# Second product of each attention score over 128 rows instead of 64, in a hybrid decoder step on Trainium2

## Chip, cores and metric

One Trainium2 chip, of which the kernel uses one core: TensorE (PE) for matrix products, VectorE (DVE), ScalarE (ACT) and GpSimd (POOL) for elementwise work, and DMA queues. The metric is the time of one execution on the device in microseconds (us). Three runs of the kernel before took 1948.69, 1954.34 and 1954.75 us; the median is 1954.34.

## The reference, cut to what matters

One layer of a decoder for 1024 prompt tokens and 8 samples of 4 tokens, model width 1024: RMSNorm, one combined projection, three parallel mixers (sliding-window attention, a gated short convolution, a gated delta net), gates and an output projection, then a gated MLP with a convolution, and a final norm. The change touches the attention of the prompt alone: 8 query heads share 2 key/value heads of 64 features, in blocks of 128 queries against 256 keys (the block's own and those of the block before):

```python
s = jnp.einsum('bnqhgd,bnkhd->bnhgqk', q, k) * (HEAD_DIM ** -0.5)
s = jnp.where(mask[None, :, None, None], s, -jnp.inf)
m = jnp.maximum(jnp.max(s, axis=-1, keepdims=True), sink)
p = jnp.exp(s - m)
p = p / (jnp.sum(p, axis=-1, keepdims=True) + jnp.exp(sink - m))
o = jnp.einsum('bnhgqk,bnkhd->bnqhgd', p, v)
```

All inputs are float32.

## The kernel before

**Products in two parts.** TensorE multiplies in float32r, which carries 12 significant bits of a number. A float32 operand is therefore split into a high and a low part (`split`, lines 215 to 218: ScalarE copies the high part, VectorE or GpSimd subtracts it from the source). A projection (`products`, line 320, matmuls on line 326) makes three products for each of 8 k tiles: w high with x high, w high with x low, w low with x high. Each product is a weight load (the operand that stays in the array, 128 x 128) and a matmul of 352 columns. Three PSUM banks serve the projections, five the other work.

**Order of the work.** A list of jobs (`ORDER`) gives the order of the projections. Between their matmuls, at every few of them, `bg.tick()` lets one of several lanes of background work issue a step: the delta net's scan, the attention, sums for later stages. A lane waits at its `yield` for a condition or an estimated time. The order of instructions on each engine is fixed when the program is built; a planner that simulates times orders them by priority (`schedule_with_timeline_sim=True`). While the program runs, an engine takes its instructions in that order, each as soon as its semaphores allow.

**The stages around the change.** Attention runs as background from about 545 to 825 us of the span, beside the projections z (of the delta net) and most of the gates. `attn_blocks` (line 1559) prepares each of the 8 blocks: it loads q and k of the block twice, into partitions 0 to 63 and 64 to 127 (lines 1571, 1572), then builds the operands. `qs` has q's high part in the upper 64 partitions (0 to 63) and q's low part in the other 64 (lines 1579, 1580). `kk[:, 0:512]` has k's high part in both halves (line 1581, ScalarE). `kk[0:64, 512:1024]` has k's low part in the first half alone (line 1582, GpSimd). Lines 1584 and 1585 do the same for v.

`units` (line 1595) are three lanes that take 16 units, one for each block and key/value head. A unit has four query heads, in two pairs; a pair shares one PSUM bank. For each head, line 1612 multiplies all 128 rows of `qs` with k's high part (q high and q low with k high in one product) and line 1613 adds the product of 64 rows, q high with k low. So a pair is a group of four matmuls with 256 columns each, with 128, 64, 128 and 64 rows. Then follow, mostly on VectorE and ScalarE, the mask (line 1616), maximum, exponentials (line 1625) and the normalisation (line 1630); TensorE transposes the result (line 1642), it is split, and line 1653 multiplies it with v. Lines 1657 and 1658 add the parts of the output, which goes to DRAM.

Behind attention, `h_build` (line 1774) prepares sums of h for the last gates in four rounds: additions on line 1789 (VectorE and GpSimd), subtractions on lines 1803 and 1812 (VectorE), and splits of the results. Line 1203 is the evacuation of projections on VectorE.

Of the kernel before, what the change touches and what calls it, by code (L numbers as in the profile page):

```python
# [7 lines left out]
F32R = mybir.dt.float32r  # L8
AF = mybir.ActivationFunctionType
ALU = mybir.AluOpType  # L10
# [4 lines left out]
D = 1024          # model width  # L15
KD = 8            # k tiles of the model width
SEQ = 1024
NB = 8            # prompt blocks (attention) and chunks (delta net) of 128 tokens
NS = 32           # sample tokens, column SEQ + b * 4 + t
T = SEQ + NS  # L20
TG = 352          # token group of one PSUM bank
# [9 lines left out]
TICK_US, UNTIL_US, DMA_US, MAX_BUSY_US = 0.45, 0.3, 2.5, 8.0   # estimates: a tick, one of a wait, a transfer's latency, a full queue  # L31
SLOT = 1084       # words of one SBUF slot
N_COL, N_BG = 24, 18
PRI_EVAC, PRI_PAIR = 100, 100
PRI_SPLIT = 200                   # how far ahead of their place in the program weights are split

# columns of the constant array
# [4 lines left out]
def shape_constants():  # L42
    """Identity, triangles and masks: they depend on the shapes alone."""
# [31 lines left out]
class Lanes:  # L75
    """Background work, traced in steps between the matrix products of the projections."""
# [10 lines left out]
    def after(self, us):  # L87
        """true us from now"""
        t = self.now + us
        return lambda: self.now >= t  # L90

    def arrived(self):
        """true when the transfers issued so far should be over"""
        return self.after(max(self.busy - self.now, 0) + DMA_US + 0.9)
# [27 lines left out]
class Arena:  # L122
    """SBUF slots of one size; a slot is free again after its tile's last use."""
# [27 lines left out]
XT_ACT = 1, 4, 7   # k tiles whose x^T the scalar engine copies  # L151
# [22 lines left out]
def trunk(tc, A, O, cst_d):  # L174
# [25 lines left out]
    def banks(n):  # L200
        """true when a lane may keep n more PSUM banks over its steps"""
        return lambda: held[0] + n <= limit[0]
# [12 lines left out]
    def split(src, hi, lo, eng):  # L215
        """hi + lo == src exactly, each in the 12 significant bits that float32r carries."""
        nc.scalar.copy(hi, src)  # L217
        eng.tensor_tensor(lo, src, f32(hi), op=ALU.subtract)  # L218
# [10 lines left out]
    # matrices of q = head * 8 + chunk: A's diagonal and off-diagonal blocks, (I + A)^-1 of the diagonal ones, U  # L229
# [20 lines left out]
    hot = cp.tile([128, 96], F32R, name="hot")      # lhsT hot[:, 46 - r:94 - r] sums into row r of 48  # L250
# [51 lines left out]
    def look():  # L302
        """The next weights, from within a step."""
        n = at["n"]
        at["n"] = n + 1
        ahead("loaded", 2, lambda j: w_load(j, jobs[j][0], jobs[j][1]))
        ahead("split", 1, w_split)
        at["n"] = n
# [11 lines left out]
    def products(ps, wh, wl, xh, xl, nk, tg):  # L320
        """ps[:, :TG] = w.T @ x over nk k tiles: float32 products of exact hi + lo parts."""
# [18 lines left out]
    def group(tg):  # L340
        """columns of the group, its prompt columns, its samples"""
        return slice(tg * TG, (tg + 1) * TG), (TG if tg < 2 else TG - NS), (0 if tg < 2 else NS)

    bt = lambda ap: ap.rearrange("p (b t) -> p b t", t=4)

    def padded(t, K):
        """[128, 8, K - 1 + 4] view of the samples' rows behind the padded prompt."""
# [3 lines left out]
    def conv(src, K, w, out):  # L351
        """Causal depthwise conv along the padded columns; out column o reads o .. o + K - 1."""
# [8 lines left out]
    def conv_samples(t, K):  # L361
        """[128, 8, 4] view of the samples' columns of a conv output."""
# [3 lines left out]
    def state_in(src, rows, nct, dst, name):  # L366
        """(rows, nct * 128) -> dst[128, nct * rows], columns (ct, row), through the tensor engine."""
# [19 lines left out]
    def state_out(src, R, nct, pr, out_p, out_s, name):  # L387
        """src[128, nct * R], per ct pr prompt rows, then the samples' rows, to the two state outputs."""
# [24 lines left out]
    # =============== h = rmsnorm(x), feature-major, as hi + lo ===============  # L413
# [36 lines left out]
    def x_group(tg):  # L450
        """Three blocks of x * ln1, feature-major, as hi + lo; 1 / rms of their tokens in rr1."""
# [49 lines left out]
    # =============== delta net: a, b, and q, k, v ===============  # L501
    kept = sb.take([128, 612 + 229])                  # the conv's states; numbers per token
    dnst, dsm = kept[:, 0:612], kept[:, 612:841]
    consts = sb.take([128, K_BM + 8 - K_TRI + 136])   # constants; the short conv's states
# [36 lines left out]
    def xT_out():  # L541
        """x feature-major, for the residual."""
# [19 lines left out]
    def ab_lane():  # L562
        """Per token: beta, g, exp of the cumulated g; rows of them for the broadcast."""
# [20 lines left out]
        # softplus(x) = max(x, 0) + log(1 + exp(-|x|))  # L584
# [26 lines left out]
    def sums(src, sa, r, acc, wait):  # L611
        """Adds the sums over the 128 partitions of src ** 2 to rows r, 16 + r, 32 + r (by token group) of acc, a
        bank and the number of rows still to come; src is dropped."""
# [13 lines left out]
    def rsqrt_rows(acc, n, out_d, scale):  # L627
        """The rows of acc to out_d: (x * scale + eps) ** -0.5."""
# [41 lines left out]
    def norm_lane():  # L670
        """l2 norm of every head's q and k over its 128 features."""
# [34 lines left out]
    def d_end(j, cb, ca):  # L706
        """Conv and silu of a tile of q, k or v before the conv."""
# [38 lines left out]
    def d_pair(j):  # L746
        """Tiles j and j + 1 of q, k, v: what takes their sums, what follows"""
# [17 lines left out]
    # =============== the delta net, in the background ===============  # L765
    h4 = lambda ap: ap.rearrange("p (h t) -> p h t", h=4)
    flat = lambda ap: ap.rearrange("p h t -> p (h t)")
    bch = lambda ap: ap.unsqueeze(1).to_broadcast([128, 4, 128])      # over heads
    bct = lambda ap: ap.unsqueeze(2).to_broadcast([128, 4, 128])      # over a head's columns
# [9 lines left out]
    def of_chunk(t, c):  # L779
        """chunk c's four heads of t[.., q = head * 8 + chunk, ..]: (row, head, col)"""  # L780
        return t.rearrange("r (h c) i -> c r h i", c=NB)[c]

    def pass1(c):
        """Per chunk: A^T = strict part of beta k k^T * decay, by blocks, and the masked q k^T * decay."""
# [43 lines left out]
    def solve():  # L828
        """(I + A)^-1 of all the 32 x 32 diagonal blocks, one block per partition (block, q)."""
# [23 lines left out]
    def merge():  # L853
        """U = (I + A)^-T of all chunks and heads: off-diagonal blocks -X22 A21 X11 of 32, then of 64,
        four or two of them along the diagonal of one matrix product; q = 16 * (upper half) + g."""
# [102 lines left out]
    def prep():  # L958
        """Per chunk: the operands of the scan."""
# [74 lines left out]
    def sample_delta():  # L1034
        """The delta rule of the samples: 128 rows (head, sequence, token) in blocks of 4."""
# [41 lines left out]
        # (I + A)^-T = (I - A^T)(I + A^T A^T): A has blocks of 4, so A^4 = 0  # L1077
# [48 lines left out]
    def out_norm():  # L1126
        """oc = rmsnorm(o) * norm_w * silu(z), feature-major."""
# [51 lines left out]
    # =============== the short convolution ===============  # L1179
# [93 lines left out]
    # =============== Strassen's recursion ===============  # L1273
    # In Winograd's form, one level: seven products of halves of the features, of the k tiles and of the tokens in
    # place of eight. A chain of products shares a PSUM bank where their sums nest.
# [14 lines left out]
    def build(bs, p, vp, vq, wait, gap=0, first=None):  # L1290
        """Operands of a pair of k tiles: hi | lo of the quarters of vp, vq and of their sums."""
# [35 lines left out]
    class Pairs:  # L1327
        """Products of pairs of weight tiles with the pieces of an operand."""
# [36 lines left out]
        def produce(self, j):  # L1365
            """hi | lo of the weights of product j % 7 of pair j // 7."""
# [36 lines left out]
        def run(self, q, bs, out, after, before=None):  # L1403
            """out(feature tile, first token, PSUM sum, another summand, whether the sum goes on)"""
# [39 lines left out]
    def summed(ps, x, more):  # L1444
        """ps + x, in a bank"""
# [6 lines left out]
    # =============== attention: q, k, v; z of the delta net; the gates ===============  # L1452
    def half_tanh(t):
        """sigmoid(x) = (tanh(x / 2) + 1) / 2; stored as tanh(x / 2)."""
# [74 lines left out]
    # =============== attention, in the background ===============  # L1529
# [21 lines left out]
    def space():  # L1551
        """Slots that the attention may take."""
# [6 lines left out]
    def attn_blocks():  # L1559
        vprev = None  # L1560
        for nb in range(NB):
# [15 lines left out]
            # q: hi over lo; k: hi twice, and lo  # L1577
# [4 lines left out]
            nc.gpsimd.tensor_tensor(kk[0:64, 512:1024], rk[0:64, 0:512], f32(kk[0:64, 0:512]), op=ALU.subtract)  # L1582
# [12 lines left out]
    def units(first, step):  # L1595
        """Softmax attention of one block and one kv head (4 query heads) at a time."""
        for u in range(first, 2 * NB, step):
# [3 lines left out]
            st, pa = lend([128, 1040])               # the scores; later the output  # L1601
# [4 lines left out]
            for hp in range(2):  # L1606
                yield banks(1)
                ps, = keep(1)
                for i in range(2):
# [3 lines left out]
                    mm(o, qs[0:64, h, :], kk[0:64, 512 + kv * 256:768 + kv * 256], start=False, stop=True)  # L1613
# [35 lines left out]
            # rows 0 .. 63: v's hi times p; rows 64 .. 127: its lo times p, added below  # L1649
# [104 lines left out]
    def attn_end():  # L1754
        yield lambda: done.get("att", 0) == 2 * NB + 1
        sb.drop(2)                                   # the constants, v's hi and lo
# [12 lines left out]
    # the last gates, in pairs  # L1769
# [4 lines left out]
    def h_build(pp):  # L1774
        """The pieces of h: its quarters where they are, the sums beside them; the last sum waits for a place."""
# [81 lines left out]
    def last_d(j):  # L1857
        """h's second quarter, back in its place."""
# [5 lines left out]
        elif j == 1:  # L1864
            for p in range(4):                        # the last sums move to free slots
# [66 lines left out]
    # =============== branches, merged; output projection ===============  # L1932
# [555 lines left out]
```

## Time and profile before

| | |
|---|---|
| median of 3 runs | 1954.34 us (1948.69 to 1954.75) |
| span of the profiled execution | 1948.5 us (the page gives no other time of it) |
| TensorE busy | 1820.2 us, 93% |
| weight loads | 1760.5 us, 90% |
| VectorE busy | 1360.4 us, 70% |
| GpSimd busy | 1017.4 us, 52% |
| ScalarE busy | 793.9 us, 41% |
| DMA | 251.24 MB, 129 GB/s |

The span is the time from the first to the last instruction of the execution that the profiler recorded. Busy times are unions of an engine's instructions. Weight loads (PEld) overlap the matmuls. A matmul's end is modelled, and matmuls overlap each other, so the distance between the starts of two of them says more than the duration of one. In the rows, L1613 is line 1613 of the kernel, `out<-in` are the program's names of tiles (`col` and `bg` are the two sorts of SBUF slots, `mm` and `bgps` the PSUM banks), and `64*128 64x256` is a product over 64 rows with 128 columns of weights and 256 moving columns.

### The profile page before, as it was taken

To read this page: it belongs to the slowest core of one execution; us is meant where nothing else is said; L and a number is where in the kernel's file an instruction comes from. 1 tells how busy PE (TensorE), PEld (TensorE's weight loads), DVE (VectorE), ACT (ScalarE), POOL (GpSimd) and SP (SyncE) were. 2 spreads that over 40 slices of the span, in tenths; PEclk is the share of its full clock that TensorE was granted. 3 is DMA by queue.
4 is the path that set the end of the run, shared out by engine and by line. 5 is a ranking of instruction groups with operands and counts; after the bars stand their busy time and mean duration, and the time that the engine had idled before them with its cause. 6 is when DMAs were issued, how large, how long until landed. Compare 5 with 4: busy or idle time off the path is not lost. (4 is left out here: it accounts for less than half of the span.)

```text
span 1948.5 us, 33487 instructions
## 1 busy us (share of the span) xinstructions
PE 1820.2 (93%) x12822; PEld 1760.5 (90%) x12822; DVE 1360.4 (70%) x2385; ACT 793.9 (41%) x1644; POOL 1017.4 (52%) x936
## 2 busy tenths in 40 slices
PE   6999899989999999989898999999999999989878
PEld 5888799989989998989787998999999999879877
DVE  5689845822447677766999757766666667986895
ACT  5654511011124444334544455545545444523312
POOL 1565666613213213363568547777777774544761
PEclk8999999988999999989999999999999999999979
DMA  6312876475745436432553342222322226512102
GB/s 218 108 60 84 286 230 192 107 192 163 228 126 152 135 101 202 166 109 96 202 179 111 121 144 88 87 79 67 99 67 83 82 67 238 190 36 100 45 12 106
DMA packets 265471, 251.24 MB, mean 129 GB/s; under 512 B 55698, under 2 KB 225150, under 8 KB 265294
## 3 DMA queue, kind: packets, MB, share of 16 engines
q1 hardware_dynamic: 209278, 208.20, 33.2%
q10 hardware_dynamic: 56032, 40.90, 7.0%
q8 instruction: 101, 1.65, 0.3%
q14 instruction: 60, 0.49, 0.1%
HBM read 176.23 MB, written 74.82 MB: 129 GB/s over the span
## 5 line engine op out<-in xcount | busy, mean ns | idle before, releaser
L326 PE MATMUL mm<-col,wh 128*128 128x352 f32 x2424 | 607.0, 329 | 17.5 <-DVE col L1203 13.7
L326 PEld LDWEIGHTS mm<-col,wh 128*128 128x128 f32 x2424 | 428.3, 191 | 26.1 <-issue 11.3
L326 PE MATMUL mm<-col,wl 128*128 128x352 f32 x1224 | 401.5, 328 | 0.0
L218 POOL TENSOR_TENSOR wl<-wr,wh 128x1024 fp32r<-128x1024 f32 x50 | 124.0, 2479 | 238.6 <-ACT wh L217 209.4
L326 PEld LDWEIGHTS mm<-col,wl 128*128 128x128 f32 x1224 | 232.9, 190 | 2.8 <-issue 0.5
L217 ACT CAST wh<-wr 128x1024 fp32r<-128x1024 f32 (+2 forms) x100 | 79.7, 803 | 178.4 <-PE mm L326 157.2
L218 POOL TENSOR_TENSOR wl<-col,wl 128x512 fp32r<-128x512 f32 (+1 forms) x78 | 101.8, 1305 | 96.2 <-ACT wl L217 89.3
L218 POOL TENSOR_TENSOR wh<-col,wh 128x512 fp32r<-128x512 f32 (+1 forms) x74 | 97.4, 1316 | 73.1 <-ACT wh L217 63.9
L1449 DVE TENSOR_TENSOR bgps<-bgps,col 128x264 f32<-128x264 f32 x136 | 59.2, 437 | 96.9 <-PE bgps L1421 91.7
L1421 PE MATMUL mm<-bg,wh 128*128 128x264 f32 x744 | 114.0, 289 | 7.4 <-DVE wh L218 2.5
L1421 PE MATMUL mm<-col,wh 128*128 128x264 f32 x648 | 105.1, 290 | 10.9 <-ACT col L1430 5.2
L1421 PE MATMUL mm<-bg,wl 128*128 128x264 f32 x720 | 109.3, 288 | 4.6 <-DVE wl L218 2.2
L1421 PEld LDWEIGHTS mm<-bg,wh 128*128 128x128 f32 x744 | 100.8, 192 | 9.5 <-DVE wh L218 2.9
L1421 PEld LDWEIGHTS mm<-bg,wl 128*128 128x128 f32 x720 | 96.9, 191 | 5.9 <-DVE wl L218 2.4
L1421 PEld LDWEIGHTS mm<-col,wh 128*128 128x128 f32 x648 | 90.4, 193 | 12.8 <-ACT col L1430 5.8
L1421 PE MATMUL mm<-col,wl 128*128 128x264 f32 x576 | 95.1, 292 | 6.8 <-POOL wl L218 3.3
L217 ACT CAST wh<-col 128x512 fp32r<-128x512 f32 (+1 forms) x86 | 48.1, 562 | 113.7 <-PE bgps L1421 59.0
L1421 PEld LDWEIGHTS mm<-col,wl 128*128 128x128 f32 x576 | 81.4, 194 | 8.0 <-POOL wl L218 3.5
L359 DVE SCALAR_TENSOR_TENSOR col<-col,vecT 128x1080 f32<-128x1080 f32 (+1 forms) x44 | 81.7, 1873 | 5.1 <-ACT col L357 3.3
L1421 PE MATMUL bgps<-col,wl 128*128 128x264 f32 x528 | 84.2, 288 | 1.0 <-POOL wl L218 1.0
L1203 DVE TENSOR_TENSOR col<-mm,bg 128x352 f32<-128x352 f32 x84 | 43.4, 517 | 56.6 <-PE mm L326 56.4
L217 ACT CAST wl<-col 128x512 fp32r<-128x512 f32 (+1 forms) x92 | 51.9, 566 | 75.1 <-PE mm L2355 32.2
(578 smaller groups left out, 4964.0 us busy)
## 6 DMA issues: line engine op xcount, KB each, us to landing
wr<-in_w_in SPq DMA_DIRECT2D x44, 512.0 KB
g_d<-col SPq DMA_DIRECT2D x24, 528.0 KB
wr<-in_ffn_up ACTq DMA_DIRECT2D x22, 512.0 KB
col<-in_ffn_up ACTq DMA_DIRECT2D x22, 512.0 KB
hid_d<-col SPq DMA_DIRECT2D x21, 512.0 KB
bg<-qkv_d SPq DMA_DIRECT2D x40, 256.0 KB
col<-g_d SPq DMA_DIRECT2D x18, 528.0 KB
col<-hid_d SPq DMA_DIRECT2D x13, 528.0 KB
```

Source lines behind the costliest of these rows:

```text
L217: nc.scalar.copy(hi, src)
L218: eng.tensor_tensor(lo, src, f32(hi), op=ALU.subtract)
L326: mm(ps[:, :TG], a[:, k, :], b[k][:, cc], start=n == 0, stop=n == last)
L359: nc.vector.scalar_tensor_tensor(out[:, :L], src[:, j:j + L], w(j), out[:, :L], op0=ALU.mult, op1=ALU.add)
L1203: nc.vector.tensor_tensor(dst[:, cc], ps[:, :TG], rr1[:, cc], op=ALU.mult)
L1421: mm(ps, w[:, x + k, :], b[y][:, c0:c0 + HU], start=not n and piece not in NESTED, stop=n == last, skip_group_check=piece in NESTED)
L1449: nc.vector.tensor_tensor(dst, ps, x, op=ALU.add)
```

## The change

The low part of k is made for all 128 partitions, so that it stands in both halves as the high part does, and the second product of each score takes all 128 rows of `qs` and of this. It then adds q high with k low, as before, and q low with k low besides. The number of matmuls, their columns and their order in the program's text stay. (The full diff also strips comments, without an effect on the program.)

```diff
             nc.scalar.copy(kk[:, 0:512], rk[:, 0:512])
-            nc.gpsimd.tensor_tensor(kk[0:64, 512:1024], rk[0:64, 0:512], f32(kk[0:64, 0:512]), op=ALU.subtract)
+            nc.gpsimd.tensor_tensor(kk[:, 512:1024], rk[:, 0:512], f32(kk[:, 0:512]), op=ALU.subtract)
...
                     mm(o, qs[:, h, :], kk[:, kc], start=True, stop=False)
-                    mm(o, qs[0:64, h, :], kk[0:64, 512 + kv * 256:768 + kv * 256], start=False, stop=True)
+                    mm(o, qs[:, h, :], kk[:, 512 + kv * 256:768 + kv * 256], start=False, stop=True)
```

## Rows read from the trace of the kernel before

**Rows 1.** The page's head and first part: busy us (share of span) and instructions.

```profile
span 1948.5 us, 33487 instructions
...
PE 1820.2 (93%) x12822; PEld 1760.5 (90%) x12822; DVE 1360.4 (70%) x2385; ACT 793.9 (41%) x1644; POOL 1017.4 (52%) x936
```

**Rows 2.** Busy us of each engine in two stretches, granted clock, DMA.

```profile
core 0: us, PE busy (x) PEld busy (x) DVE busy (x) ACT busy (x) POOL busy (x), PEclk, DMA share, GB/s
570.00:800.00 230.00, 230.00 (x1376) 208.29 (x1375) 157.14 (x271) 99.93 (x232) 54.89 (x33) 1.00 0.52 157
...
800.00:850.00 50.00, 50.00 (x317) 49.46 (x315) 41.24 (x46) 18.94 (x32) 29.31 (x13) 1.00 0.33 106
```

**Rows 3.** Matmuls of lines 1612, 1613: ns min/median/max, first and last start us.

```profile
L1612 PE MATMUL bgps<-col x32: 278/382/385, 574.3 to 682.9; 128*128 128x256 f32 x32
...
L1613 PE MATMUL bgps<-col x32: 379/382/382, 574.6 to 683.3; 64*128 64x256 f32 x32
...
L1613 PE MATMUL bgps<-bg x24: 379/382/384, 701.9 to 796.1; 64*128 64x256 f32 x24
```

**Rows 4.** TensorE in order of time, second and last group: start, duration us.

```profile
577.37 0.32 PE L326 MATMUL mm<-col,wl 128*128 128x352 f32 x1
577.53 0.28 PE L1612 MATMUL bgps<-col 128*128 128x256 f32 x1
577.74 0.38 PE L1613 MATMUL bgps<-col 64*128 64x256 f32 x1
578.05 0.38 PE L1612 MATMUL bgps<-col 128*128 128x256 f32 x1
578.37 0.38 PE L1613 MATMUL bgps<-col 64*128 64x256 f32 x1
578.68 0.59 PE L326 MATMUL mm<-col,wh 128*128 128x352 f32 x2
579.10 0.32 PE L326 MATMUL mm<-col,wl 128*128 128x352 f32 x1
...
795.27 0.28 PE L1612 MATMUL bgps<-bg 128*128 128x256 f32 x1
...
796.42 0.43 PE L326 MATMUL mm<-col,wl 128*128 128x352 f32 x1
```

**Rows 5.** Weight loads in order of time, same group [idle before, ended by].

```profile
577.38 0.19 PEld L1612 LDWEIGHTS bgps<-col 128*128 128x128 f32 x1
577.74 0.18 PEld L1613 LDWEIGHTS bgps<-col 64*128 64x128 f32 x1 [0.17 <-issue]
```

**Rows 6.** TensorE in order of time: full-row products of 256 and 264 columns.

```profile
730.80 0.28 PE L1612 MATMUL bgps<-bg,col 128*128 128x256 f32 x1
730.91 0.33 PE L326 MATMUL mm<-col,wh 128*128 128x352 f32 x1
...
1300.03 0.89 PE L1421 MATMUL mm<-bg,col 128*128 128x264 f32 x6
1300.76 0.52 PE L1421 MATMUL mm<-col 128*128 128x264 f32 x3
```

**Rows 7.** GpSimd's subtraction, line 1582 (min/median/max); one of 128 partitions (busy, mean).

```profile
L1582 POOL TENSOR_TENSOR col<-bg,col x4: 1287/1548/2274, 558.4 to 667.6; 64x512 fp32r<-64x512 f32 x4
...
L973 POOL TENSOR_TENSOR bg<-bg 128x512 f32<-128x512 f32 x3 | 3.9, 1284 | 0.0
```

**Rows 8.** Waits of TensorE, 850 to 862 us (total, times, longest); VectorE, GpSimd around 815.

```profile
PE mm L326 <- DVE col L1203: 9.1, 1, 9.1
...
814.52 0.69 DVE L218 TENSOR_TENSOR bg<-bgps,bg 128x512 fp32r<-128x512 f32 x1 [0.48 <-ACT bg L217]
815.12 2.48 DVE L1789 TENSOR_TENSOR bg<-col 128x1056 f32<-128x1056 f32 x1
...
814.08 2.41 POOL L218 TENSOR_TENSOR wl<-wr,wh 128x1024 fp32r<-128x1024 f32 x1 [9.93 <-ACT wh L217]
```

**Rows 9.** VectorE's normalisation and TensorE's first transposes of unit 0.

```profile
594.50 1.22 DVE L1630 TENSOR_TENSOR col<-col 128x1024 f32<-128x1024 f32 x1
...
596.48 0.60 PE L1642 MATMUL bgps<-ident,col 128*128 128x128 f32 x4
```

## The prediction

> **What bounds the kernel now.** The page's head comes first: TensorE is busy 93% of a span of 1948.5 us, the next engine, VectorE, 70% [rows 1]. The share is a mean, so the stage of the change is read by itself. The second products of line 1613 (two for each of 8 blocks, 2 k/v heads and 2 pairs of query heads, 64) lie between 574.6 and 796.1 us [rows 3]; the busy times of that stretch, 570 to 800 us, give TensorE 230.00 of 230 us at a granted clock of 1.00, which is 2.4 GHz, VectorE 157, ScalarE 100, GpSimd 55 [rows 2]. TensorE has no gap there: what shortens its own sequence there moves everything behind it, as long as no other engine falls behind.
>
> Busy time doesn't say how tight the sequence is, since matmuls overlap; start-to-start times do. In the timeline, four score products (128 rows, 64 rows, 128, 64) start at 577.53, 577.74, 578.05 and 578.37, and the next projection product at 578.68 [rows 4]. So a group takes 1.15 us, with three of its steps at 0.31, although a 352-column product just before takes a step of 0.16 (577.37 to 577.53) with more columns. The weight loads tell why. The load for the full-row score product starts at 577.38, during the projection product that starts at 577.37, and 0.15 us ahead of its own product. The load for the 64-row product starts at 577.74, after an idle time of 0.17 us marked as "issue", together with its own product [rows 5]. In this trace, then, a load isn't taken ahead when the number of rows changes between it and the product in front, in either direction: the step from 64 rows back to 128 (578.05 to 578.37 is a step into 64 rows, 578.37 to 578.68 one out of them; into 64 rows behind a load that was early it is 0.21, 577.53 to 577.74) is as long. The projection behind pays too: the two products from 578.68 take 0.42 us to 579.10 where two steps of 0.16 would be 0.32.
>
> **The change part by part.** *The matmuls.* Their number, order and columns stay; the second product of each score has 128 rows in place of 64. There are 64 of them in 32 groups, the last from 795.27 to 796.42, again 1.15 us [rows 3, 4]; most groups are of 1.14 or 1.15, three of 1.23, and a few are interleaved with other work. Before: 32 x 1.15 = 36.8 us. After, all steps are between full-row products of 256 columns. The trace has one: a score product at 730.80 is followed by a projection product at 730.91, a step of 0.11; the 264-column products of a later stage need 0.73 us for six, 0.122 each [rows 6]. I take 0.12, being between these and nearer to the many than to the one: 32 x 4 x 0.12 = 15.4 us. That is 21.4 less. The 0.10 behind each group goes as well, since the next load is of as many rows: 32 x 0.10 = 3.2. Sum: 24.6 us of TensorE's own sequence.
>
> The bounds: the most is 0.11 a step, 36.8 + 3.2 - 14.1 = 25.9. The other end is that full-row products that add into the same bank in pairs don't overlap: this trace has no pair of them of 256 columns, and at 0.31 a step nothing is saved; at the end further out, time that grows with the rows, the sum has the other sign (a rival). I stand by the near rows: the 264-column products also add into one bank one after the other.
>
> The Trainium skill, "TensorE: Matmul & The Clock Gate", section "The mechanism", has a rule against this change: a weight load overlaps running matmuls "only when row_grp differs", which would leave full-row loads waiting just as now and the sum at zero. The loads of [rows 5] differ from it: the full-row load at 577.38 runs beside a full-row product, and it is the change of rows that isn't overlapped.
>
> *The subtraction on GpSimd* (line 1582) makes k's low part for 128 partitions in place of 64, eight times. Its 64-partition form takes 1287 ns at the least, and a 128 x 512 subtraction of the same engine 1284 ns on average [rows 7]: no difference. Were it to double, it would be 8 x 1.3 = 10 us more on an engine that is idle for 175 of the stretch's 230 us, with the block's first score product many us behind (block 0: subtraction from 558.4, first score at 574.3 [rows 3, 7]); nothing on the path. It reads nothing new that arrives later: line 1572 already loads k into both halves, and line 1581, for which it waits today, already writes the high part of all 128 rows in one instruction. So no wait, DMA or buffer is added, and nothing is moved past a queue.
>
> *What is late next.* TensorE comes to later work sooner, so each dependency that was covered has less cover. In a unit of attention the transposes follow the normalisation; tightest is unit 0: normalised until 595.72, transposed from 596.48, a margin of 0.76 us [rows 9]. Two score groups lie between its last score and the transposes, so TensorE comes 2 x 0.77 = 1.5 us earlier: about 0.8 us of waiting. In the same two views the other fifteen units have more. VectorE goes from 157/230 to 157/205 = 77%, below the 41.2/50 = 82% which it has from 800 to 850 while TensorE still has no gap [rows 2].
>
> The next large wait is 9.1 us, on VectorE's line 1203 at 859 [rows 8]. Before it, sums of h for the last gates are built by VectorE, ScalarE and GpSimd in four rounds from 815 to 859, 44 us that a faster TensorE doesn't shorten. What counts is what starts them: VectorE's first instruction of them at 815.12 follows at once on a subtraction that waits for ScalarE's copy of transposes, and GpSimd's follows on a weight split that had waited 9.93 us for ScalarE's part [rows 8], which waits for a weight buffer that TensorE's projection frees. Both are paced by TensorE, so the rounds move forward with it and the wait stays at about 9 us. Behind it the stages are the same work. I take off 1.2 us for waits: 24.6 - 1.2 = 23.4 us.
>
> The span would be 1925.1. The page gives no other time of the profiled execution; the runs shown are 1948.69, 1954.34 and 1954.75, so the span lies 0.2 under the lowest and 5.8 under the median. I forecast against the median: 1954.3 - 23.4 = 1931 us.
>
> **The rivals.** *The gain is partly eaten by the other engines.* If the rounds of 815 to 859 start only half as much earlier, because VectorE and GpSimd are still busy with attention's last units, the wait at 859 grows by some 12 us and half the gain is left: 1954 - 12 = 1942. For it: VectorE's 82% from 800 to 850 [rows 2], and that the 9.1 us wait is on VectorE [rows 8]. Against it: VectorE waits on ScalarE just ahead of 815.
>
> *No overlap, or all eaten.* Consecutive full-row products with different weights in one group keep 0.31 a step, or the wait at 859 grows by the whole gain to about 33 us: 1954. For the first: no row shows a pair of 256-column score products. Against: [rows 6].
>
> *Slower: the time of the second product goes with its rows.* If the 64-row step were 0.31 because 64 rows are half of 128, the full one would be 0.62: 64 x 0.31 = 19.8 us more, 1974. It decides from a mean step above 0.335 us over the 128 products (36.8 + 5.9 = 42.7, over 128; 0.29 now). Against it: 64-row products have the median of 382 ns, as have the 128-row ones of the first 32, whose least is 278 [rows 3]; rows don't set the time.
>
> *The order comes out otherwise.* The order of instructions is made by a planner that simulates times; should 128 rows cost it something else, lanes shift: 1925 to 1960, a little more likely below.
>
> **How the numbers follow.** Under 0.3% (5.9 us) a measurement of this kernel can't be told from no change. Forecast 0.70 (own range 1925 to 1937: 0.11 to 0.13 a step, up to 6 us of waits, and the spread of the runs); half eaten 0.12; none left 0.09; slower by rows 0.04; other order 0.05, of which 0.03 faster. Faster 0.70 + 0.12 + 0.03 = 0.85; same 0.09 + 0.01 = 0.10; slower 0.05. The range from 1923 to 1945 takes in the forecast, the half case and some of the last, and leaves out those at 1954 and 1974.
>
> **What would show it.** Right: line 1613 has products of 128 x 256 starting 0.12 us after the one in front, groups of about 0.47 us, weight loads ahead of their products, and no long first step behind a group; TensorE still without gaps from 570 to about 775; attention's last scores near 772 in place of 796; the 9 us wait near 836. Wrong: steps still of 0.31 (no overlap) or 0.6 (rows), a wait at the end of the rounds of 20 us and more, new waits of TensorE on VectorE within attention, or the subtraction on GpSimd near 2.6 us with score products waiting for it.

## The result, and the profile after

Four runs of the changed kernel took 1922.36 to 1930.53 us, the median 1930.22, beside 1952.49 us for the kernel before (four runs). The ratio is 0.9882 with a 95% interval of 0.9860 to 0.9905: 22.3 us less (18.5 to 27.3 by the interval), against 23.4 forecast. The profiled execution took 1930.07 us, 1.9 more than its span.

The head of the page after (busy us, share of span, instructions):

```profile
span 1928.2 us, 33489 instructions
...
PE 1795.5 (93%) x12822; PEld 1752.2 (91%) x12822; DVE 1363.0 (71%) x2385; ACT 792.6 (41%) x1644; POOL 1020.2 (53%) x936
```

TensorE does the same number of matmuls in 24.7 us less, and its weight loads are busy for 8.3 us less; no other engine changes by more than 3 us. Every engine has the same instructions in the same order. They differ in the rows of line 1613 on TensorE and the partitions of line 1582 on GpSimd, which also waits for two more semaphores (33489 instructions in place of 33487). So the two traces can be laid side by side, instruction by instruction.

Attention's stretch, in busy us by engine, then the second products (ns min/median/max, first and last start in us), against [rows 2, 3]:

```profile
core 0: us, PE busy (x) PEld busy (x) DVE busy (x) ACT busy (x) POOL busy (x), PEclk, DMA share, GB/s
...
570.00:775.00 205.00, 205.00 (x1374) 201.35 (x1374) 152.97 (x265) 97.85 (x224) 54.44 (x34) 1.00 0.56 172
```

```profile
L1613 PE MATMUL bgps<-col x32: 278/283/283, 576.9 to 673.6; 128*128 128x256 f32 x32
...
L1613 PE MATMUL bgps<-bg x24: 278/283/285, 691.8 to 774.1; 128*128 128x256 f32 x24
```

TensorE still has no gap, and 1374 matmuls, nearly as many as before (1376), fill 205 us in place of 230. The weight loads are busy for 201 of the 205 us; before, 208 of 230. One group on TensorE, then its weight loads (start us, duration us), against [rows 4, 5]:

```profile
578.99 0.32 PE L326 MATMUL mm<-col,wl 128*128 128x352 f32 x1
579.15 0.28 PE L1612 MATMUL bgps<-col 128*128 128x256 f32 x1
579.27 0.28 PE L1613 MATMUL bgps<-col 128*128 128x256 f32 x1
579.39 0.28 PE L1612 MATMUL bgps<-col 128*128 128x256 f32 x1
579.51 0.28 PE L1613 MATMUL bgps<-col 128*128 128x256 f32 x1
579.63 0.49 PE L326 MATMUL mm<-col,wh 128*128 128x352 f32 x2
579.95 0.32 PE L326 MATMUL mm<-col,wl 128*128 128x352 f32 x1
```

```profile
579.00 0.19 PEld L1612 LDWEIGHTS bgps<-col 128*128 128x128 f32 x1
579.15 0.19 PEld L1613 LDWEIGHTS bgps<-col 128*128 128x128 f32 x1
579.27 0.19 PEld L1612 LDWEIGHTS bgps<-col 128*128 128x128 f32 x1
579.39 0.19 PEld L1613 LDWEIGHTS bgps<-col 128*128 128x128 f32 x1
```

The load of a second product now starts at 579.15, with the product in front of it, and 0.12 us ahead of its own. The group takes 0.48 us (579.15 to 579.63) where it took 1.15, and the two products behind it take 0.32 (579.63 to 579.95) where they took 0.42.

The wait behind attention, as TensorE's waits from 825 to 840 us (total, times, longest), against [rows 8], and in the timeline, where the first row is of the kernel before:

```profile
PE mm L326 <- DVE col L1203: 8.8, 1, 8.8
```

```profile
859.38 0.92 PE L326 MATMUL mm<-col,wh 128*128 128x352 f32 x2 [9.08 <-DVE col L1203]
...
837.09 0.93 PE L326 MATMUL mm<-col,wh 128*128 128x352 f32 x2 [8.84 <-DVE col L1203]
```

```profile
792.85 2.48 DVE L1789 TENSOR_TENSOR bg<-col 128x1056 f32<-128x1056 f32 x1
```

It ends at 837.1 in place of 859.4 and is as long as before within 0.3 us. VectorE's first instruction of the rounds of sums starts at 792.85 in place of 815.12: the rounds that TensorE waits for moved forward with it, by the same 22.3 us. (This profile was 2.4 us late before attention began, so 24.7 us gained there leave 22.3.)

### The profile page after: what moved, and what is told of

It reads as the page before. It is cut to its first block, busy times and chain, and to the rows that moved or that the text cites. A ratio compares the mean times of both kernels' runs of the same rounds, so it can differ in the third digit from the quotient of the medians.

```text
span 1928.2 us, 33489 instructions
## 1 busy us (share of the span) xinstructions
PE 1795.5 (93%) x12822; PEld 1752.2 (91%) x12822; DVE 1363.0 (71%) x2385; ACT 792.6 (41%) x1644; POOL 1020.2 (53%) x936
## 5 line engine op out<-in xcount | busy, mean ns | idle before, releaser
L1421 PE MATMUL bgps<-bg,wl 128*128 128x264 f32 x504 | 75.8, 286 | 3.5 <-DVE col L1999 2.7
```

Of the source, the lines that this page charges most:

```text
L1421: mm(ps, w[:, x + k, :], b[y][:, c0:c0 + HU], start=not n and piece not in NESTED, stop=n == last, skip_group_check=piece in NESTED)
```

## The experiments

**The subtraction alone.** Is it TensorE's 64 rows, or GpSimd's 64 partitions?

```diff
-            nc.gpsimd.tensor_tensor(kk[0:64, 512:1024], rk[0:64, 0:512], f32(kk[0:64, 0:512]), op=ALU.subtract)
+            nc.gpsimd.tensor_tensor(kk[:, 512:1024], rk[:, 0:512], f32(kk[:, 0:512]), op=ALU.subtract)
```

> Only GpSimd's subtraction covers 128 partitions; the second products stay at 64 rows. Theory (the gain is TensorE's: a weight load isn't taken ahead when the number of rows differs from the product in front): groups stay at 1.15 us, time as before, 1952 us within 0.3%, the subtraction as long as before (least about 1.28 us). Rival (the subtraction over 64 partitions was itself what held the scores back, or the wider one costs time): a time that moves by several us, down if 64 partitions were slow, up by as much as 10 us if 128 take twice as long and the scores wait for it.

Ratio to before 0.9999 (0.9984 to 1.0013). The subtraction's durations and a group, from that kernel's trace:

```profile
L1582 POOL TENSOR_TENSOR col<-bg,col x4: 1294/1676/2279, 559.6 to 668.8; 128x512 fp32r<-128x512 f32 x4
```

```profile
578.74 0.28 PE L1612 MATMUL bgps<-col 128*128 128x256 f32 x1
578.95 0.38 PE L1613 MATMUL bgps<-col 64*128 64x256 f32 x1
579.26 0.38 PE L1612 MATMUL bgps<-col 128*128 128x256 f32 x1
579.57 0.38 PE L1613 MATMUL bgps<-col 64*128 64x256 f32 x1
579.88 0.59 PE L326 MATMUL mm<-col,wh 128*128 128x352 f32 x2
```

The subtraction takes 1294 ns at the least against 1287 with 64 partitions, and a group takes 1.14 us. The gain is the matmuls'; the subtraction has no part in it that an interval of 0.15% to either side would show.

**Half the changes of rows.** The same products, the two full ones first. (Only the first opens the bank; the second full one writes its half without.)

```diff
-                for i in range(2):
-                    h = 4 * kv + 2 * hp + i
-                    o = ps[:, i * 256:(i + 1) * 256]
-                    mm(o, qs[:, h, :], kk[:, kc], start=True, stop=False)
-                    mm(o, qs[0:64, h, :], kk[0:64, 512 + kv * 256:768 + kv * 256], start=False, stop=True)
+                for rows, kcs in ((128, kc), (64, slice(512 + kv * 256, 768 + kv * 256))):
+                    for i in range(2):
+                        h = 4 * kv + 2 * hp + i
+                        o = ps[:, i * 256:(i + 1) * 256]
+                        mm(o, qs[0:rows, h, :], kk[0:rows, kcs], start=rows == 128 and not i, stop=rows == 64 and i == 1,
+                           skip_group_check=True)
```

> The four products of a pair in the order 128, 128, 64, 64 rows in place of 128, 64, 128, 64; the same products, half the changes of the number of rows. Theory (each change costs, both ways): steps of 0.12 between the two full ones and 0.12 between the two of 64 rows, 0.2 to 0.31 into the 64 rows, 0.31 out of them and 0.10 behind; a group of about 0.8 us in place of 1.15, 11 us less in all, 1941 us, if the planner's order does not shift much else (it does shift, so the steps in the trace count for more than the total). Rival (a 64-row product is slow by itself, whatever stands in front): the step between the two 64-row products stays at 0.3, the group at about 1.0 us and the time at 1948 or more.

1943.82 us, ratio 0.9951 (0.9934 to 0.9968), 9.6 us less than before. A group in its trace (the four score products merge into one row, with the rows of the first), and what follows; then the second 64-row product and its weight load by themselves:

```profile
579.46 0.82 PE L1613 MATMUL bgps<-col 128*128 128x256 f32 x4
580.21 0.59 PE L326 MATMUL mm<-col,wh 128*128 128x352 f32 x2
580.64 0.32 PE L326 MATMUL mm<-col,wl 128*128 128x352 f32 x1
```

```profile
580.00 0.28 PE L1613 MATMUL bgps<-col 64*128 64x256 f32 x1
...
579.89 0.19 PEld L1613 LDWEIGHTS bgps<-col 64*128 64x128 f32 x1
```

The group takes 0.75 us, and the two products behind it 0.43. In size, that sides with the theory. So does the second 64-row product: its load starts 0.11 us ahead of it, and it takes 0.28 us, as a full one, where a 64-row product behind a full one takes 0.38. Within the group the expectation missed: the medians of the start-to-start times in the trace are 0.117 (full to full), 0.209 (full to 64), 0.223 (64 to 64) and 0.207 (64 to full). The step between two 64-row products is not 0.12. What fits the steps of both kernels is that a change costs about 0.19 us, half in the step into the changed product and half in the next one, as behind every group: before, four changes cost 1.15 - 0.48 + 0.10 = 0.77 a group; here two cost 0.75 - 0.48 + 0.11 = 0.38.

**96 rows.** Is it any change of the number of rows, or only one of the part of the array in use?

```diff
-            nc.gpsimd.tensor_tensor(kk[0:64, 512:1024], rk[0:64, 0:512], f32(kk[0:64, 0:512]), op=ALU.subtract)
+            nc.gpsimd.tensor_tensor(kk[0:96, 512:1024], rk[0:96, 0:512], f32(kk[0:96, 0:512]), op=ALU.subtract)
...
-                    mm(o, qs[0:64, h, :], kk[0:64, 512 + kv * 256:768 + kv * 256], start=False, stop=True)
+                    mm(o, qs[0:96, h, :], kk[0:96, 512 + kv * 256:768 + kv * 256], start=False, stop=True)
```

> The second products and the subtraction over 96 rows in place of 64 (it adds q low with k low for half of the features). Theory A (any change of the number of rows stops the early load): groups stay at 1.15 us, time as before, 1952 us. Theory B (only a change of the part of the array that is used, 64 rows being half and 96 not, stops it): groups of 0.47 us, time as after, 1930 us. Nothing in between is expected of either.

1929.57 us, ratio 0.9882 (0.9858 to 0.9907), the same as the full change. A group in its trace, and the only row in the view of TensorE's waits from 540 to 830 us:

```profile
579.16 0.28 PE L1612 MATMUL bgps<-col 128*128 128x256 f32 x1
579.28 0.28 PE L1613 MATMUL bgps<-col 96*128 96x256 f32 x1
579.40 0.28 PE L1612 MATMUL bgps<-col 128*128 128x256 f32 x1
579.52 0.28 PE L1613 MATMUL bgps<-col 96*128 96x256 f32 x1
579.64 0.49 PE L326 MATMUL mm<-col,wh 128*128 128x352 f32 x2
```

```profile
PE bgps L1016 <- ACT bg L1010: 1.8, 1, 1.8
```

A group takes 0.48 us although the rows go 128, 96, 128, 96: a change between 128 and 96 rows costs nothing, one between 128 and 64 does. So theory A, which is how the prediction put it ("when the number of rows changes"), falls, and what B forecast came in. Its reason, the part of the array in use, is not seen in a trace by itself, and other numbers of rows were not tried among these products. The Trainium skill, "TensorEngine Tiling (Array Packing)", sections "Available Configurations" and "Key Properties", says that the array has modes of 128, 64 and 32 rows and that going from one to another drains TensorE; 96 rows without a cost and 64 with 0.19 us a change agree with that, if 96 rows count as the mode of 128.

**Without the second products.** What do they still cost? This kernel leaves out the product of q high with k low.

```diff
-                    mm(o, qs[:, h, :], kk[:, kc], start=True, stop=False)
-                    mm(o, qs[0:64, h, :], kk[0:64, 512 + kv * 256:768 + kv * 256], start=False, stop=True)
+                    mm(o, qs[:, h, :], kk[:, kc], start=True, stop=True)
```

> The second products are left out (no q high with k low), 64 matmuls less. Theory: what a full-row second product still costs is its step of 0.12 us, so against the changed kernel 64 x 0.12 = 7.7 us less: groups of 0.24 us, about 1922 us, less what a kernel order that differs in places moves. Rival (the steps of the second products are hidden in the changed kernel, TensorE being held by other engines in this stretch): the time stays at 1930 us. If it fell by 20 us or more against the changed kernel, the second products would still cost more than their steps.

1920.39 us, ratio 0.9828 (0.9811 to 0.9845), 9.2 us under the kernel with 96 rows in the same rounds. A group in its trace:

```profile
574.26 0.40 PE L1612 MATMUL bgps<-col 128*128 128x256 f32 x2
574.50 0.32 PE L326 MATMUL mm<-col,wl 128*128 128x352 f32 x1
```

The group takes 0.24 us for its two products. Summed from each score product's start to the next matmul's, the trace has 7.8 us here and 15.5 in the changed kernel: the 64 products cost the 7.7 us of their steps, and the rest of the 9.2 is within what the intervals leave open. So the time still follows TensorE's matmuls in this stretch after the change.

**Again, both kernels.** In the first pair of profiles the changed kernel gains a lead of 24.7 us across attention, of which 22.7 are left at the end. Is the difference a loss behind attention?

> The changed kernel once more, for a second profile. In the first pair of profiles the lead over the kernel before is 24.7 us where attention ends and at the wait of 8.8 us behind it, 19.2 us at 1067 us, 22.7 us at the end (from an instruction just ahead of the scores on). Theory: what moves between 940 and 1100 us and near 1700 us is the spread between executions of stages held by VectorE, not a loss that the change brings: the lead at the end of attention is 24 to 25 us again (step of 0.12, groups of 0.47), the stage from 840 to 1070 us differs by 2 us or more from that of the first profile. Rival (the earlier arrival costs some 5 us there each time): the same stage is as long as in the first profile within 0.5 us.

> The kernel before once more, for a second profile. Theory (spread of the stages held by VectorE): the stretch behind attention up to 1100 us is 2 us or more longer or shorter than in the first profile of the same kernel, with attention itself equal within 0.5 us. Rival (the stretch is the same each time and the change made it longer): equal within 0.5 us.

The changed kernel's ratio was 0.9870 (0.9854 to 0.9887), the kernel before took 1948.77 us in its one run. Here is how much later (+) or earlier (-) than in the first profile of the kernel before TensorE gets through three stretches, from the starts of the same instructions. The stretches are in times of that first profile; the wait, which ends there at 859.4, lies in the second one. (The last row but one is a third profile of the changed kernel, from the rounds below.)

| us | attention, 562 to 839 | 839 to 1066 | 1644 to the end |
|---|---|---|---|
| before, second profile | +0.6 | +2.6 | -5.5 |
| subtraction alone | 0.0 | +2.0 | -1.5 |
| changed | -24.7 | +5.5 | -3.5 |
| changed, second profile | -24.3 | +3.9 | -0.6 |
| changed, third profile | -24.2 | +2.2 | -5.1 |
| 96 rows | -22.4 | +2.7 | -0.3 |

Attention repeats within 0.6 us, the later stretches don't repeat within several. Neither expectation is met to the letter for the changed kernel (the stretch from 839 differs by 1.6 us, between the 2 and the 0.5 named); for the kernel before the spread is met, at 2.6, and the 0.5 us within which attention was to repeat is missed by 0.1. With 0 to 2.6 without the change and 2.2 to 5.5 with it, a loss of 1 or 2 us there is neither shown nor excluded.

**Towards a faster version.** What is left behind attention is the wait of 8.8 us on four rounds of sums. Two edits of the changed kernel tried to shorten it: the lane of the sums one projection earlier, and one split of each round on VectorE.

```diff
- g00 g01 g02 g03 g04 g05 g06 hb g07 g20 pairs g21 G22 op1 G24 G26
+ g00 g01 g02 g03 g04 g05 hb g06 g07 g20 pairs g21 G22 op1 G24 G26
```

> The changed kernel, with the lane that builds the sums for the last gates added one projection earlier. Theory: the wait of 8.8 us behind attention is as long as four rounds of additions and splits take beyond TensorE's work beside them, and starts with the room that attention leaves; if the lane gets its slots earlier, the wait gets shorter by up to 8.8 us and the time falls to 1922 us at best. Rival: the slots come free only with the last units, so the lane starts where it did: 1930 us within 0.3%.

```diff
-            put("t3", b12, nc.gpsimd)
+            put("t3", b12, nc.gpsimd if pp is dpp else nc.vector)
```

> The changed kernel, with one of the three splits of each round of these sums moved from GpSimd to VectorE. Theory (each round waits for GpSimd: VectorE idles 3.15 to 3.6 us before the next round until GpSimd's last split is done): a round gets 1 to 2 us shorter, the wait of 8.8 us falls to 2 to 6 us and the time to 1923 to 1927 us. Rival (the rounds are held by GpSimd's additions and its splits of weights, which stay): the wait stays and the time is 1930 us within 0.3%, or VectorE's longer queue makes it worse.

TensorE's waits from 800 to 840 us, of the first, then of the second:

```profile
PE mm L326 <- DVE col L1203: 18.0, 1, 18.0
```

```profile
PE mm L326 <- DVE col L1203: 6.7, 3, 3.1
```

The first took 1939.2 us (0.9930, 0.9914 to 0.9947), slower than the changed kernel: the wait doubled. Neither side had expected that. VectorE's evacuations of projections in this stretch, in the changed kernel, then in this one, show what TensorE waits for:

```profile
814.20 0.51 DVE L1203 TENSOR_TENSOR col<-mm,bg 128x352 f32<-128x352 f32 x1
819.03 0.52 DVE L1203 TENSOR_TENSOR col<-mm,bg 128x352 f32<-128x352 f32 x1
821.44 0.53 DVE L1203 TENSOR_TENSOR col<-mm,bg 128x352 f32<-128x352 f32 x1
836.43 0.94 DVE L1203 TENSOR_TENSOR col<-mm,bg 128x352 f32<-128x352 f32 x2
```

```profile
808.71 0.51 DVE L1203 TENSOR_TENSOR col<-mm,bg 128x352 f32<-128x352 f32 x1
...
831.55 0.94 DVE L1203 TENSOR_TENSOR col<-mm,bg 128x352 f32<-128x352 f32 x2
```

The rounds start where they did (790.54 against 792.85, in a profile that is 2.3 us ahead before attention too), but between 808.71 and 831.55 VectorE has no evacuation, where the changed kernel has three: they now stand behind the rounds, and TensorE waits for the first of them.

The second took 1923.5 us (0.9851, 0.9833 to 0.9870) beside 1927.77 for the changed kernel. These two once more in five rounds:

> The changed kernel, beside the next one in five rounds each. Theory: 0.987 to 0.988 of the time before, 1926 to 1930 us. Rival (half of the gain lies in lucky executions): 0.992 or more.

> The changed kernel with one split of each round moved to VectorE, once more. In the first profile the wait behind attention fell from 8.8 to 6.7 us in three pieces, and TensorE came 7 to 9 us earlier to the stage behind. Theory (that lead is kept, less what the spread of the stage takes): 4 us less than the changed kernel in the same rounds, 0.985 of the time before. Rival (the lead is given back in the stages held by VectorE, which has more to do): the same time as the changed kernel within 2 us.

The changed kernel 1925.29 us (0.9859, 0.9834 to 0.9884), the one with the split moved 1919.96 us (0.9837, 0.9815 to 0.9859). It was the lower both times, by 4.3 and 5.3 us, with 6.7 and 5.2 us left of the wait; but the intervals overlap, and at 0.2 to 0.3% it can't be called faster for certain.

## Why the prediction was right

**The sum.** 36.8 us for the 32 groups before were 36.77 in the trace (from each score product's start to the next matmul's). 15.4 after are 15.47: steps of 0.12, from the 264-column row that was nearest. The 0.10 behind each group is 0.16 in place of 0.265 us from the first product behind it to the second, in the 28 of 32 groups where that first one is a projection's; the other four lose as much or more. Together 24.6 us, and the lead across attention was 24.7, 24.3 and 24.2 in three executions.

**What is late next.** The 0.8 us of waiting in unit 0 did not come. VectorE's normalisation and TensorE's transposes of that unit, against [rows 9], with a subtraction ahead of the normalisation; and the same subtraction before:

```profile
586.73 1.22 DVE L1580 TENSOR_TENSOR col<-bg,col 64x1024 fp32r<-64x1024 f32 x1
...
593.40 1.23 DVE L1630 TENSOR_TENSOR col<-col 128x1024 f32<-128x1024 f32 x1
```

```profile
595.78 0.60 PE L1642 MATMUL bgps<-ident,col 128*128 128x128 f32 x4
```

```profile
586.77 3.41 DVE L1580 TENSOR_TENSOR col<-bg,col 64x1024 fp32r<-64x1024 f32 x1
```

The margin is 1.15 us (1.15 to 1.17 in three profiles of the changed kernel), where 0.76 was to shrink. The 0.76 rested on one execution: the second profile of the kernel before has 0.14, that of the subtraction alone 1.18. The prediction let the normalisation move by the two groups of unit 0 alone. Counted from that unit's first score product, the transposes come 3.1 us earlier (19.1 us behind it in place of 22.2), which is four groups, but the normalisation ends 3.5 us earlier (17.9 in place of 21.4): VectorE idles 0.3 us in between in place of 2.7, and its subtraction on line 1580 takes 1.22 us in place of 3.41. Why the subtraction got shorter was not followed. The prediction had no ground for it, so that the margin held is in part luck. That a cover can go is seen in the kernel with 96 rows, whose matmuls have the same spacing: its lead across attention is 2.3 us smaller than the first one's, and 2.1 of them go at its wait of 1.8 us on ScalarE. The 1.2 us taken off for waits stand for nothing that the changed kernel's traces show: from 540 to 825 us TensorE waits for nothing in two of them and 0.2 us in the third, and the wait behind attention did not grow. The 24.6 us of the sum are borne out by the lead across attention; that 23.4 came within 1.1 us of the measured 22.3 is luck, since by the medians of three comparisons the gain was 22.3, 24.2 and 27.8 us.

**The wait behind attention** kept its length (8.8 to 9.1 us in five profiles of the two kernels) and moved with attention's end, as foreseen; "half eaten" and "all eaten" fall by it. The rule that a weight load overlaps only where row groups differ, of the Trainium skill's "TensorE: Matmul & The Clock Gate", section "The mechanism", would have kept the step at 0.31; it is 0.12, and the loads start a product ahead. (The same section also lets a load into the background weight buffer run ahead, and that is not at odds with these steps.) The rival of time that grows with the rows falls by the 283 ns and the steps of 0.12 us at 128 rows, and by 0.12 at 96. The planner's order did not change.

**What was off.** The mechanism was named too broadly: not any change in the number of rows, but one into or out of the 64-row use of the array. The sum didn't depend on it, since it took its steps from full-row products. And the base was shaky: the profiled execution's time is 1.9 us above its span (1930.07 and 1928.2), so by an estimate the one of before stands at 1950.4, not next to the lowest run, and the kernel before had medians of 1952.0 to 1953.4 us in later rounds, the changed one of 1925.3 to 1930.2. In the rival of the rows, 42.7 over 128 is 0.334, not 0.335; nothing hangs on it.

## What to carry to other kernels

Here a product over 64 rows among products over 128 is not cheaper but dearer: 0.19 us for each change in or out, against 0.12 us for a whole full-row product of 256 columns. Where TensorE is the bound and the operands can be filled up (with a copy as here, or with zeros, which was not tried), one size for all products is the better choice; where they can't, products of one size should stand together. Look for weight loads that start with their own product, not with the one in front. The matmuls' busy share doesn't show them (all of the stretch, before and after); the weight loads' share does so only in part (91% before, 98% after).

## What the runs showed of the hardware that was not expected

A product over 96 rows goes as one over 128: steps of 0.12 us between them, in both directions. Two 64-row products one behind the other were 0.22 us apart, which the delayed half of the change before them accounts for; whether a long run of 64-row products would go at 0.12 was not tried. The kernel before has a run of ten products over 40 rows, with 8 columns each, and the next product behind it:

```profile
57.08 1.28 PE L568 MATMUL bgps<-bg 40*128 40x8 f32 x10
58.29 0.43 PE L326 MATMUL mm<-col,wl 128*128 128x352 f32 x1
```

They take 1.21 us, 0.12 each with the change at their end: fewer rows by themselves bring no 0.19 us for each product.

GpSimd's subtraction of 512 columns takes the same over 64, 96 and 128 partitions within 1%: 1287, 1290 and 1293 ns at the least, for the form of [rows 7].
